# A hybrid encoder layer on one core: G leaves in quarters of a stage, and two stages of it stay in SBUF

## The chip, the cores and the metric

The kernel runs on one core of a Trainium2 chip. The metric is the device time in microseconds (us) of one execution, lower is better; the median of three runs before the change is 1501.55 us (1500.29 to 1506.06). The engines are TensorE (PE, matmuls), VectorE (DVE), ScalarE (ACT), GpSimd (POOL) and SyncE (SP, which here only issues transfers). ScalarE and GpSimd issue transfers too, each on a queue of its own, and all queues share the core's 16 DMA engines.

## The reference, cut to what matters

One encoder layer over 512 tokens of width 1024: layer norm, two kinds of attention, an output projection, layer norm, and then PEER, a feed-forward layer that picks experts by product keys. The change touches PEER alone.

```python
q = (xb @ w_q).reshape(PEER_CHUNK, PEER_HEADS, PEER_KEY_DIM)
s1 = jnp.einsum('thd,kd->thk', q[..., :half], sub_keys[0])
s2 = jnp.einsum('thd,kd->thk', q[..., half:], sub_keys[1])
...                      # top 16 of each, top 16 of the 16 x 16 sums
idx = (e1 * PEER_N_KEYS + e2)            # 128 experts a token, of 16384
g = jax.nn.softmax(cv, axis=-1)
u = u_table[idx]
act = g * gelu(jnp.einsum('td,ted->te', xb, u))
return jnp.einsum('te,ted->td', act, v_table[idx])
```

U and V have 16384 rows of 1024 floats. A last layer norm follows.

## The kernel before, in words

The 512 tokens are four chunks of 128. Chunk 0 is done **by gathers**: for each of its 128 picks, GpSimd gathers a row of U per token into a tile (`gat`, eight buffers), VectorE multiplies it with h and sums (`gather_u`, line 1564, into the scratch tile `scr`), and later the same with rows of V (`gather_v`, line 1575).

Chunks 1 to 3 are done **densely**: the table is taken as 128 blocks of 128 experts. Per block, `hidden = gelu(h @ U_block)`, times a dense weight matrix G, and the product times `V_block` is summed in PSUM over all blocks (`expert_out`, line 1590). G has one weight for each token and expert, mostly zeros. It is built from one-hot matrices: for eight tokens at a time VectorE and ScalarE write one-hot tiles (`oh_i`, `oh_j`), PE multiplies them, and ScalarE copies the products from PSUM into a **stage tile** `g_st` of 32 tokens (128 partitions x 128 blocks x 32 tokens, 16 KB a partition, 2 MB in all). There are two stage tiles, `bs0` and `bs1`, used in turn. A full stage goes to `g_dram` in DRAM by one write issued on ScalarE's queue (lines 1124 and 1199). Chunks 2 and 3 are built by `build_g_split` (fp16, line 1075), chunk 1 last by `build_g` (line 1158). That makes twelve stages. Only the very last one (chunk 1, group 3) is not written: its tile `bs1` is kept and later read from SBUF.

Chunk 1 needs more than G: its 128 tokens are `own` tokens, whose hidden values are also had by gathers (`rows`, line 1237 the gather, line 1239 the product, in place, with five row buffers). These rows run beside the building of G.

**The order** is written out by hand. While G is built, PE also multiplies the first 104 blocks of U (`lead_block`, line 1349, tile `whole` holds h transposed) and the gate matrix. A generator `pe_work` yields this PE work in small pieces, and `run` (line 1458) goes through the steps of a builder: after each step that costs VectorE time it puts in as much PE work as fits (`run_pe`), and some rows (`own`). Every engine then works its own list in order. SP's list holds the loads of U blocks, of gate weights, the first load of G back from DRAM (line 1502, for eight blocks of experts and chunks 2 and 3), and then the loads of V blocks.

In the **last stage** (from about 903 us) each of the 128 blocks needs its V block, split in a high and a low part, and its piece of G: `load_g` (line 1517) fetches eight blocks of G at a time, in four loads of three 32-token groups each (`q` = 0 to 3); for `q` = 1 the group that stayed in `bs1` is copied by ScalarE (line 1527) and only two groups are loaded. The gathers of chunk 0 run beside it.

SBUF is full, so where tiles lie matters: a tile in a place that was used before waits for the last user of that place. After G is built, `pb.close()` frees `bt` (the one-hots) and `bs0`; the pools `pV` (V blocks, half of G's pieces) and `pO` (`a_hi`, `a_lo`, the two parts of the weighted hidden values) take this place from the inner end, so that `a_hi`, `a_lo` and the first V tile lie where `bs0` was. `pR.close()` frees the routing tiles, the row buffers and `raw_u`; `pG` (`scr` and the eight `gat`) takes their place. `whole` lies in a pool of its own and keeps its place to the end.

## Time and profile before

| | us |
|---|---|
| median of three runs | 1501.55 |
| fastest, slowest | 1500.29, 1506.06 |
| the profiled execution | 1503.96 |
| its span in the profile | 1502.0 |
| PE busy | 1464.8 |
| DVE busy | 1288.5 |
| ACT busy | 632.8 |
| POOL busy | 571.2 |

The times below are those of one profiled execution, counted from the start of its span. In a table by stage the columns are: the stage, its length, the busy time of each engine with its instructions, the clock that PE was granted (1.00 is full), the mean share of time in which the DMA engines were busy, and GB/s moved. In a timeline the columns are start, length, engine, line and operation, with the idle time ahead of it and what ended it in brackets. In a list of waits: who waited for whom, us in total, times, the longest. In a list of transfers: size and median us from issue to landing. The building of G covers about 490 to 900 us; its writes leave at 515, 537, 565 and 590 us (chunk 2), 748, 770, 797 and 813 us (chunk 3), 841, 862 and 877 us (chunk 1).

### The profile page before, as it was taken

The page shows a single profiled execution, that of the slowest core. Times are in us where ns is not written, and L with a number is a line of the kernel's source. Part 1 is how long each engine was busy: PE and PEld are TensorE (multiplying, and loading weights), DVE is VectorE, ACT ScalarE, POOL GpSimd, SP SyncE. Part 2 cuts the span into 40 slices and gives each one's busy share as a digit, 9 for nine tenths or more (in the row PEclk, how much of TensorE's full clock was granted, in tenths as well). Part 3 has the DMA queues.
Part 4 walks back from the last instruction along what each step waited for, and adds up shares of the span by engine and source line. Part 5 has one row for each costly group of instructions (what it writes and reads, how often), then busy time and mean ns, then how long its engine had stood idle before and what let it go on. Part 6 is the DMA issues. An engine that isn't in the chain of part 4 may idle for free.

```text
span 1502.0 us, 22685 instructions
## 1 busy us (share of the span) xinstructions
PE 1464.8 (98%) x7725; PEld 1231.3 (82%) x7725; DVE 1288.5 (86%) x2830; ACT 632.8 (42%) x1175; POOL 571.2 (38%) x520
## 2 busy tenths in 40 slices
PE   9999999999999989999999999999999999999997
PEld 5788777788888878788888988888988888888885
DVE  7376786579998979998767989999989999999997
ACT  3355676243221654212555663444434333333433
POOL 1013110010014544334432335555645666666630
PEclk9999999999999999999999999999999999999999
DMA  7343341175339999999999999999999999999992
GB/s 252 98 113 97 87 119 36 29 242 168 99 135 353 349 415 378 389 323 339 393 418 386 364 385 371 417 415 415 418 401 383 411 412 412 411 412 413 411 385 85
DMA packets 192294, 455.82 MB, mean 303 GB/s; under 512 B 18225, under 2 KB 96049, under 8 KB 190770
## 3 DMA queue, kind: packets, MB, share of 16 engines
q1 hardware_dynamic: 119936, 212.63, 38.7%
q0 software_dynamic: 57984, 207.12, 35.4%
q10 hardware_dynamic: 14258, 34.61, 5.9%
q8 instruction: 61, 1.00, 0.2%
q14 instruction: 55, 0.45, 0.1%
HBM read 412.62 MB, written 38.80 MB: 301 GB/s over the span
## 4 chain that ended last, share of the span: by engine, by line
PE 46%; issue 8%; DVE 6%; POOL 6%; DMA 4%; ACT 1%; POOLq 0%; ACTq 0%; DVEq 0%
PE acc L1590 34%; PE mm L1349 4%; DMA whi<-in_u_rows_dram,s_ix 3%; POOL whi L1237 2%; POOL wlo L1237 2%; PE hp L131 2%; PE hp L130 2%; PE hp L129 2%; PE tr L1178 1%; POOL row L1237 1%; PE hp L1349 1%; DMA g_dram<-g_st 1%; DVE whi L1239 1%; DVE wlo L1239 1%; DVE ci L887 0%
## 5 line engine op out<-in xcount | busy, mean ns | idle before, releaser
L1573 POOL DMA_INDIRECT gat<-in_v_rows_dram,i_sel x128 | 207.5, 1621 | 110.9 <-DVE base L1575 86.9
L1558 POOL DMA_INDIRECT gat<-in_u_rows_dram,i_sel x102 | 135.2, 1325 | 112.1 <-DVE hdot L1564 79.7
L110 ACT CAST a_hi<-gt 128x384 fp32r<-128x384 f32 (+2 forms) x128 | 65.0, 509 | 264.7 <-DVE gt L1640 162.8
L1575 DVE SCALAR_TENSOR_TENSOR base<-gat,hdot,base 128x1024 f32<-128x1024 f32 x128 | 163.9, 1280 | 1.8
L110 DVE TENSOR_TENSOR wlo<-raw,whi 128x1024 fp32r<-128x1024 f32 (+4 forms) x113 | 131.5, 1164 | 39.4 <-ACT whi L110 38.9
L110 ACT CAST whi<-raw 128x1024 fp32r<-128x1024 f32 (+4 forms) x113 | 113.0, 1001 | 90.6 <-PE mm L130 47.3
L1349 PE MATMUL mm<-whole,raw 128*128 128x256 f32 x656 | 149.2, 381 | 0.0
L1237 POOL DMA_INDIRECT whi<-in_u_rows_dram,s_ix x51 | 64.2, 1259 | 223.4 <-DVE cand L993 129.7
L1590 PE MATMUL acc<-hTh,a_hi 128*128 128x512 f32 x480 | 148.8, 390 | 0.0
L1590 PE MATMUL acc<-hTl,a_hi 128*128 128x512 f32 x480 | 148.6, 390 | 0.1
L1590 PE MATMUL acc<-hTh,a_lo 128*128 128x512 f32 x480 | 148.4, 389 | 0.0
L1349 PEld LDWEIGHTS mm<-whole,raw 128*128 128x128 f32 x656 | 122.9, 190 | 15.6
L1564 DVE CUSTOM_DVE_ANT_0 scr<-gat,h 128x1024 f32<-128x1024 f32 x102 | 124.6, 1222 | 2.0
L1590 PEld LDWEIGHTS acc<-hTl,a_hi 128*128 128x128 f32 x480 | 90.0, 188 | 19.5 <-DVE hTl L110 0.5
L1590 PEld LDWEIGHTS acc<-hTh,a_lo 128*128 128x128 f32 x480 | 90.1, 188 | 18.9
L110 ACT CAST hTh<-v_raw 128x1024 fp32r<-128x1024 f32 x78 | 81.9, 1050 | 55.3 <-PE acc L1590 19.9
L1590 PEld LDWEIGHTS acc<-hTh,a_hi 128*128 128x128 f32 x480 | 88.4, 188 | 17.1 <-ACT a_hi L110 0.2
L110 DVE TENSOR_TENSOR hTl<-v_raw,hTh 128x1024 fp32r<-128x1024 f32 x78 | 95.0, 1219 | 5.4 <-ACT hTh L110 5.4
L1237 POOL DMA_INDIRECT wlo<-in_u_rows_dram,s_ix x51 | 60.7, 1191 | 68.4 <-DVE s_dot L1239 55.8
L1590 PE MATMUL acc<-whi,a_hi 128*128 128x512 f32 x276 | 85.0, 389 | 0.0
L1590 PE MATMUL acc<-wlo,a_hi 128*128 128x512 f32 x276 | 85.0, 389 | 0.0
L1590 PE MATMUL acc<-whi,a_lo 128*128 128x512 f32 x276 | 84.9, 389 | 0.0
(414 smaller groups left out, 3524.0 us busy)
## 6 DMA issues: line engine op xcount, KB each, us to landing
v_raw<-in_v_rows_dram SPq DMA_DIRECT2D x82, 512.0 KB, 12.7
raw<-in_uT_dram SPq DMA_DIRECT2D x81, 512.0 KB, 8.2
g_dram<-g_st ACTq DMA_DIRECT2D x11, 2048.0 KB, 12.5
raw<-in_v_rows_dram SPq DMA_DIRECT2D x44, 512.0 KB, 13.3
gt<-g_dram SPq DMA_DIRECT2D x45, 384.0 KB, 13.7
ge_dram<-ge ACTq DMA_DIRECT2D x88, 128.0 KB, 6.9
ge<-ge_dram SPq DMA_DIRECT2D x88, 128.0 KB, 13.1
raw_u<-in_uT_dram SPq DMA_DIRECT2D x18, 512.0 KB, 7.5
```

Of the source, the lines that this page charges most:

```text
L110: cut = nc.scalar.copy(hi, src), nc.vector.tensor_tensor(lo, src, r32(hi), op=OP.subtract)
L129: nc.tensor.matmul(ps, a[0], b[0], start=start, stop=False)
L130: nc.tensor.matmul(ps, a[0], b[1], start=False, stop=False)
L131: nc.tensor.matmul(ps, a[1], b[0], start=False, stop=stop)
L1237: nc.gpsimd.indirect_dma_start(out=u[:], out_offset=None, in_=u_rows, in_offset=bass.IndirectOffsetOnAxis(ap=ix[:, k:k + 1], axis=0))
L1239: nc.vector.tensor_tensor_reduce(u, u, x, op0=OP.mult, op1=OP.add, accum_out=dots[:, k:k + 1], scale=1.0, scalar=0.0)
L1349: nc.tensor.matmul(ps[:, :N_U], raw[:, k], whole[:, k, :], start=(k == 0), stop=(k == 7))
L1558: nc.gpsimd.indirect_dma_start(out=u[:], out_offset=None, in_=u_rows, in_offset=bass.IndirectOffsetOnAxis(ap=i_sel[:, c, k:k + 1], axis=0))
L1564: nc.vector.tensor_tensor_reduce(scr, u, h[c], op0=OP.mult, op1=OP.add, accum_out=hdot[:, c, k:k + 1], scale=1.0, scalar=0.0)
L1573: nc.gpsimd.indirect_dma_start(out=u[:], out_offset=None, in_=v_rows, in_offset=bass.IndirectOffsetOnAxis(ap=i_sel[:, c, k:k + 1], axis=0))
L1575: nc.vector.scalar_tensor_tensor(base[c], u, hdot[:, c, k:k + 1], base[c], op0=OP.mult, op1=OP.add)
L1590: nc.tensor.matmul(acc[c][hf], a[:, cs], b[:, hf * 512:(hf + 1) * 512], start=(n == 0 and i == 0), stop=(n == 127 and i == 2))
```

## The change

- **Writes in quarters.** A finished stage is no longer written at once. Its four quarters (32 of the 128 blocks each, 512 KB, 4 KB a partition) go on a list, and a new function `send` issues one at the head of each step of `run`. What is left on the list is issued before the first load of G back, and once more at the end of the building.
- **Two stages stay.** Groups 2 and 3 of chunk 1 stay in `bs0` and `bs1`. `load_g` copies one of them for `q` = 0 and the other for `q` = 1, and loads two groups instead of three for both.
- **Places.** `bs0` is now kept to the end like `bs1` and lies beside it, so `bt` lies further in. `whole` is freed with the routing tiles. To that end the rest of `pe_work` is put in ahead of `pR.close()` (and of the first V loads). `pV` opens after it.
- **Gather tiles.** `scr` is gone: `gather_u` writes its product over the gathered row, and the last layer norms use a gather tile. The eight tiles are now 4 `gat`, 2 `gat_w` (where `whole` was) and 2 `gat_v`, taken in a fixed order: four, two, two. The two rows of layer-norm parameters at the end are loaded into `gat`.

The core of the diff:

```diff
+G_PARTS = 4
...
-    pW = ctx.enter_context(tc.tile_pool(name="pW", bufs=1, reuse_waits="tile"))
+    pR = ExitStack()
+    pW = pR.enter_context(tc.tile_pool(name="pW", bufs=1, reuse_waits="tile"))
     whole = pW.tile([128, 8, N_U], F32, name="whole")
...
+    bs = [ctx.enter_context(tc.tile_pool(name="bs0", bufs=1, side="right", reuse_waits="tile")), bs1]
     bt = pb.enter_context(tc.tile_pool(name="bt", bufs=2, side="right", reuse_waits="tile"))
-    bs = [pb.enter_context(tc.tile_pool(name="bs0", bufs=1, side="right", reuse_waits="tile")), bs1]
...
+    parts = []
+
+    def send():
+
+        if parts:
+            g, t, x = parts.pop(0)
+            n = 128 // G_PARTS
+            nc.scalar.dma_start(g_dram[g][:, x * n * GT:(x + 1) * n * GT],
+                                t[:, x * n:(x + 1) * n].rearrange("p i t -> p (i t)"))
...
-                if c == NGC and g == N_S // GT - 1:
+                if c == NGC and g >= N_S // GT - 2:
                     g_last.append(stage)
                 else:
-                    nc.scalar.dma_start(g_dram[g], stage.rearrange("p i t -> p (i t)"))
+                    parts.extend((g, stage, x) for x in range(G_PARTS))
...
         for amount in steps:
+            send()
...
+        while parts:
+            send()
         first_g = pX.tile([128, NTG, GB, GT], F32, name="gt1")
...
         for x in own:
             run_pe(x)
+        while parts:
+            send()
         pb.close()
...
-        g = slice(q * NTG // 4 + (q == 1), (q + 1) * NTG // 4)
-        if q == 1:
-            nc.scalar.copy(t[:, N_S // GT - 1], g_last[0][:, i:i + GB, :])
+        g = slice(q * NTG // 4 + (q == 1), (q + 1) * NTG // 4 - (q == 0))
+        if q < 2:
+            nc.scalar.copy(t[:, N_S // GT - 2 + q], g_last[q][:, i:i + GB, :])
...
+    with tc.manual_schedule(engines={nc.vector.engine, nc.scalar.engine, nc.tensor.engine, nc.sync.engine,
+                                     nc.gpsimd.engine}):
+        gating = True
+        for _ in pe_work:
+            pass
     pR.close()
...
-    scr = pG.tile([128, D], F32, name="scr")
+    def gat():
+        nonlocal n_gat
+        name, n = (("gat", GATS - 4), ("gat_w", 2), ("gat_v", 2))[max(0, n_gat % GATS // 2 - 1)]
+        n_gat += 1
+        return pG.tile([128, D], F32, name=name, bufs=n)
...
-        nc.vector.tensor_tensor_reduce(scr, u, h[c], op0=OP.mult, op1=OP.add, accum_out=hdot[:, c, k:k + 1],
+        nc.vector.tensor_tensor_reduce(u, u, h[c], op0=OP.mult, op1=OP.add, accum_out=hdot[:, c, k:k + 1],
```

## The prediction

> **What bounds the kernel now.** I read the page first, then busy time by stage, then the engine waits inside the stages that have idle time, then the transfers in flight there.

> ```profile
> span 1502.0 us, 22685 instructions
> PE 1464.8 (98%) x7725; PEld 1231.3 (82%) x7725; DVE 1288.5 (86%) x2830; ACT 632.8 (42%) x1175; POOL 571.2 (38%) x520
> ```

> TensorE is busy for 98% of the span, and the change takes no matmul away. All there is to win is the 37 us in which PE stands still, and the time in which it runs at a lower clock. The stages from the first write of G on:

> ```profile
> core 0: us, PE busy (x) PEld busy (x) DVE busy (x) ACT busy (x) POOL busy (x), PEclk, DMA share, GB/s
> 515.00:540.00 25.00, 25.00 (x164) 21.89 (x162) 18.04 (x30) 16.55 (x41) 11.18 (x9) 1.00 1.00 399
> 540.00:555.00 15.00, 10.08 (x63) 8.72 (x62) 8.51 (x14) 4.99 (x11) 4.25 (x4) 0.89 1.03 420
> ...
> 600.00:615.00 15.00, 14.08 (x63) 11.32 (x62) 13.16 (x51) 1.80 (x4) 3.82 (x4) 1.00 1.03 412
> ...
> 780.00:795.00 15.00, 11.90 (x55) 9.85 (x53) 10.71 (x17) 6.71 (x17) 5.96 (x5) 0.77 1.02 404
> ...
> 884.00:903.00 19.00, 16.48 (x93) 13.65 (x92) 14.48 (x36) 10.79 (x25) 5.62 (x7) 1.00 0.94 378
> 903.00:1480.00 577.00, 577.00 (x2814) 488.65 (x2814) 558.05 (x744) 225.25 (x316) 334.30 (x223) 1.00 1.01 398
> ```

> From 903 on PE never stops, so whatever is won before 903 arrives at the end in full. PE's idle time is 4.92 us in 540-555, 0.92 in 600-615, 3.10 in 780-795 and 2.52 in 884-903. The clock adds to it: 15 us at 0.89 lose 1.65, 15 us at 0.77 lose 3.45. Together 16.6 us, and that is the ceiling of the gain. The stalls themselves, in PE's timeline:

> ```profile
> 541.80 1.04 PE L1105 MATMUL tr<-oh_i,oh_j 128*128 128x128 f16 x15 [1.70 <-DVE oh_j L1144]
> ...
> 551.78 1.78 PE L1105 MATMUL tr<-oh_i,oh_j 128*128 128x128 f16 x15 [3.22 <-DVE oh_j L1144]
> ...
> 787.29 0.29 PE L1105 MATMUL tr<-oh_i,oh_j 128*128 128x128 f16 x1 [2.79 <-DVE oh_j L1144]
> ```

> PE waits for one-hot products of VectorE. VectorE is late because, in order, it first multiplies rows of U that GpSimd gathers (L1239), and these arrive late. Its waits in 515-555, then in 750-790:

> ```profile
> DVE whi L1239 <- DMA whi<-in_u_rows_dram,s_ix: 5.5, 4, 3.4
> DVE row L1239 <- DMA row<-in_u_rows_dram,s_ix: 5.2, 2, 4.9
> DVE wlo L1239 <- DMA wlo<-in_u_rows_dram,s_ix: 2.7, 3, 1.6
> ```
> ```profile
> DVE wlo L1239 <- DMA wlo<-in_u_rows_dram,s_ix: 5.6, 4, 3.8
> DVE whi L1239 <- DMA whi<-in_u_rows_dram,s_ix: 4.9, 4, 1.9
> DVE row L1239 <- DMA row<-in_u_rows_dram,s_ix: 1.5, 1, 1.5
> ```

> That is 13.4 and 12.0 us of lateness, of which PE felt 4.92 and 3.10: about 8.5 us are absorbed by VectorE's lead over PE. Time from issue to landing, one line each from the transfers of 500-515 (before the first write of G), then from those of 520-550 and 740-790 (with such writes):

> ```profile
> whi<-in_u_rows_dram,s_ix POOLq DMA_INDIRECT x4, 6.1
> ```
> ```profile
> whi<-in_u_rows_dram,s_ix POOLq DMA_INDIRECT x4, 15.0
> ```
> ```profile
> g_dram<-g_st ACTq DMA_DIRECT2D x2, 2048.0 KB, 12.9
> ...
> whi<-in_u_rows_dram,s_ix POOLq DMA_INDIRECT x7, 12.9
> ```

> A row takes 6.1 us in the quiet and 13 to 15 beside the writes. The last stall, at 884-903, is of another kind:

> ```profile
> 877.25 0.33 ACTq L1199 DMA_DIRECT2D g_dram<-g_st  x1
> ...
> 889.71 0.41 ACT L110 CAST a_hi<-gt 128x256 fp32r<-128x256 f32 x1 [5.00 <-DMA g_dram<-g_st]
> ```
> ```profile
> 890.15 0.43 DVE L110 TENSOR_TENSOR a_lo<-gt,a_hi 128x256 fp32r<-128x256 f32 x1 [2.81 <-ACT a_hi L110]
> ```
> ```profile
> 892.01 2.53 PE L1178 MATMUL tr<-oh_i,oh_j 128*128 128x128 f32 x16 [1.19 <-ACT g_st L1191]
> ...
> 898.23 1.17 PE L1178 MATMUL tr<-oh_i,oh_j 128*128 128x128 f32 x8 [1.00 <-DVE oh_j L1220]
> ```

> The tile of a_hi lies where stage tile bs0 was, so ScalarE stands 5.0 us until the last 2 MB of G have left bs0; the copies out of PSUM queue behind it, and PE loses 2.4 us.

> **The change part by part.**

> *The last stall.* Group 2 of chunk 1 is no longer written, bs0 stays, and pO and pV move to where raw_u, row and bt were. Those are read for the last time by 878 (PE, raw_u), by 886 (VectorE, row) and, for bt, by the last products. So nothing holds a_hi after 878: the 5.0 us go, and with them 2.2 of the 2.52 us. The v loads, in SP's order

> ```profile
> 889.74 10.52 SPq L1543 DMA_DIRECT2D v_raw<-in_v_rows_dram  x3
> ```

> start with the first at about 886 instead of 889.74 and the others with the last products, as now; PE needs them only after the two blocks that are cut early. The tail of pe_work that now stands ahead of them issues nothing on SP any more. Gain 2.2 us, bounds 1.5 and 2.5.

> *Four writes for one.* 11 writes become 40: one 512 KB quarter at the head of each of the next four steps. The bytes fall by one stage.

> ```profile
> DMA packets 192294, 455.82 MB, mean 303 GB/s; under 512 B 18225, under 2 KB 96049, under 8 KB 190770
> ```

> Only 1524 packets are 8 KB or more, 1408 of them (11 x 128) these writes, at 16 KB; rows of U and V go in 4 KB. How far do the rows profit? Lower bound, nothing: the engines are full (399 to 420 GB/s in the stages above, no less than the 398 of the last stage), and what is full is not sped up by cutting it smaller. Upper bound, all 14.0 us (6.57 + 0.92 + 6.55). Between them: 2.10 MB in 12.9 us are 163 GB/s, 39% of 417; three queues served alike would leave a write a third, 139. The 24 GB/s set free go mostly to the rows. How fast these go, from VectorE's time on line 1239 (two instructions a row) between the writes and in 724-748, where VectorE was ahead and PE set the pace:

> ```profile
> 515.00:552.50 37.50, 14.13 (x24) 0.99 1.01 406
> 724.00:748.00 24.00, 13.48 (x22) 1.00 1.01 395
> ```

> 12 rows in 37.5 us, one in 3.1 or 168 GB/s, where PE asks for one in 2.2. With 24 GB/s more it is one in 2.7: the lateness per row falls from 0.9 to 0.5 us, by some 40%. It does not vanish, but since 8.5 of 13.4 us are absorbed already, a fall by 37% (4.92 of 13.4) in the first set and by 26% (3.10 of 12.0) in the second is enough to keep PE running. The writes themselves may end later: each stage tile has a whole stage of time. I take 65% of the two large stalls with their clock, 0.65 x 13.1 = 8.5 us, and half of the 0.92, because the estimate stands only just above the threshold.

> [...]

> [...]

> *ScalarE issues 29 more writes.*

> ```profile
> L1124 ACTq DMA_DIRECT2D g_dram<-g_st x8: 326/326/327, 515.5 to 813.3; - x8
> ```

> 29 x 0.33 = 9.5 us on ScalarE, which is 66% busy in 515-540 and mostly waits for PE. Behind a quarter queue its share of the one-hots and the copies out of PSUM. Cost 0 to 3 us; I take 0.8, since no engine waits for ScalarE in the large stalls. There is a second wait in it. The program hands the transfers of SP and ScalarE eight completion semaphores in turn, so an issue waits for the eighth before it, which SP already shows on loads of U that touch neither tensor:

> ```profile
> SPq L1309 <- DMA ge_dram<-ge: 3.2, 1, 3.2
> SPq L1309 <- DMA g_dram<-g_st: 2.8, 1, 2.8
> ```

> With four quarters inside one round of eight tokens, that eighth is, by my estimate from the rate of loads and writes, about 9 us old instead of 16. This is rival 3.

> *The first load of G back (L1502)* waits for all writes of chunks 2 and 3.

> ```profile
> SPq L1502 <- DMA g_dram<-g_st: 8.4, 1, 8.4
> ```
> ```profile
> 826.15 0.38 SPq L1502 DMA_DIRECT2D gt<-g_dram  x1
> 826.62 1.01 SPq L1309 DMA_DIRECT2D raw<-in_uT_dram  x2
> ```

> The last stage's first quarter leaves at 813.3 as now, the other three only after the lag of lead blocks, at about 818. No gathers run there, the same bytes remain, so I expect the load at 826 to 828. Behind it queue two loads of U, the first needed about 2 us after it lands. Cost 0 to 3 us, I take 0.5.

> *The rest costs nothing.*

> ```profile
> L1564 DVE CUSTOM_DVE_ANT_0 scr<-gat,h 128x1024 f32<-128x1024 f32 x102 | 124.6, 1222 | 2.0
> L1239 DVE CUSTOM_DVE_ANT_0 whi<-whi,h_s 128x1024 f32<-128x1024 f32 x51 | 62.1, 1218 | 18.2 <-DMA whi<-in_u_rows_dram,s_ix 18.2
> L1527 ACT COPY gt<-g_st 128x256 f32<-128x256 f32 x15 | 6.0, 402 | 1.6 <-DVE a_lo L110 1.3
> ```

> Writing the product over u instead of scr: 1218 against 1222 ns, the in-place form being L1239's. 15 more copies of 402 ns lie on ScalarE in the last stage, 39% busy (225 of 577); if PE were to wait for them it would be 6 us. 15 loads of G shrink by a third, which PE does not feel. The fifth and sixth gathers now wait for PE's last reading of whole (about 896) and the eighth for h_s as now; their products are due after 910, a landing of 8 us fits.

> *Sum:* 2.2 + 8.5 + 0.5 - 0.8 - 0.5 = 9.9 us. The profiled execution took 1503.96 us, 1502.0 of span and 1.96 around it, 2.4 above the median of 1501.55. From its own time the sum gives 1494.1, on the scale of the median **1491.7**.

> **The rivals.**
> 1. *The rows are freed wholly.* 16 KB packets are the whole cause; landing falls to 6-8 us, all 16.6 us come back, less 1.3 for issues: 1486.2. For it: 6.1 against 15.0. Against: the landing stays long at full bandwidth.
> 2. *The DMA engines are simply full.* Rows stay at 13 us, PE stalls as before at 550 and 787, and only the 2.2 us less 1.3 remain: 1500.7. For it: 399-420 GB/s. Against: writes may be late and rows may not.
> 3. *Slower: ScalarE blocks on completions.* A quarter, in order, waits for a transfer 9 us old; at the landing of 12.9 it waits 3.9 us, 31 us over the eight stages of chunks 2 and 3. It decides once wait and issues in a stage exceed ScalarE's idle third, some 7 us of 21. Then the stalls of today remain and each set gets another like them: +13.1 - 2.2 = 1512.5.

> **How the numbers follow.** Forecast 0.48, rival 1 0.13, rival 2 0.29, rival 3 0.10. What a measurement of this kernel tells from no change is about 0.5%, 7.5 us: faster is below 1494.0, slower above 1509.1. The forecast's own range is 1487 to 1496, three quarters of it below 1494: 0.36 + 0.13 + 0.02 of rival 2 = 0.51 faster; slower 0.08 of rival 3; 0.41 the same. The range 1485 to 1503 holds forecast, rivals 1 and 2 and leaves out rival 3.

> **What would show it.** In the profile after: rows of U landing at about 11 us beside the quarters; no PE wait above 2 us and a clock of 1.00 in the stages that stood at 0.89 and 0.77; no ScalarE wait for g_dram before a_hi; PE at the last stage some 10 us earlier than 903. I am wrong if rows still take 13 us and more, if ScalarE's queue shows waits for transfers, or if PE gets idle time after it enters the last stage.

## The result and the profile after

| | before | after |
|---|---|---|
| median | 1501.85 | 1492.91 |
| fastest, slowest of six runs | 1500.29, 1506.06 | 1491.66, 1495.41 |
| the profiled execution, its span | 1503.96, 1502.0 | 1492.1, 1490.3 |
| ratio with its 95% interval | | 0.9939 [0.9924, 0.9954] |

The changed kernel is 8.9 us faster. The prediction was 1491.7 in a range of 1485 to 1503. The head of the page after:

```profile
span 1490.3 us, 22670 instructions
...
PE 1459.5 (98%) x7725; PEld 1228.6 (82%) x7725; DVE 1285.3 (86%) x2830; ACT 635.5 (43%) x1190; POOL 575.5 (39%) x520
```

Between the two profiled executions lie 11.7 us of span. To place them, first busy time from 490 us to the stage's end, before and then after (columns as in the prediction):

```profile
490.00:1480.00 990.00, 975.43 (x5100) 835.48 (x5099) 909.68 (x1512) 416.20 (x764) 500.59 (x366) 0.99 1.00 389
```
```profile
490.00:1468.30 978.30, 969.77 (x5094) 832.41 (x5093) 903.46 (x1509) 417.18 (x773) 503.16 (x364) 1.00 0.99 388
```

PE idles 14.57 us in the first and 8.53 in the second: **6.0 us less idle time**. The rest is clock. In stretches of 5 us, before:

```profile
550.00:555.00 5.00, 3.22 (x19) 2.94 (x20) 3.95 (x7) 1.58 (x3) 1.95 (x2) 0.66 1.04 413
...
785.00:790.00 5.00, 2.39 (x17) 2.13 (x18) 4.19 (x7) 0.89 (x2) 1.88 (x3) 0.70 1.03 416
790.00:795.00 5.00, 5.00 (x16) 4.08 (x15) 4.42 (x8) 2.26 (x7) 3.15 (x3) 0.62 1.00 380
```

and after:

```profile
555.00:560.00 5.00, 4.55 (x25) 3.97 (x26) 4.04 (x8) 4.16 (x12) 1.49 (x2) 0.66 1.03 415
```

While G is built, before loses 1.7 us of clock at 550 and 1.5 + 1.9 at 785, after only 1.7 at 555: **3.4 us less loss**. About 1.7 us more come from the clock in the stretch at 175 to 190, long before the change acts (0.94, 0.50 and 0.88 before, one 0.67 after); the two executions merely differ there. So 6.0 + 3.4 = 9.4 us belong to the change, beside 8.9 in the medians. The last 0.6 us lie before 490 as well, in PE's idle time there (12.83 and 12.28 us).

What PE waits for in 490 to 905, before and after:

```profile
PE tr L1105 <- DVE oh_j L1144: 9.3, 5, 3.2
PE tr L1178 <- ACT g_st L1191: 1.5, 2, 1.2
...
PE tr L1178 <- DVE oh_j L1220: 1.2, 2, 1.0
```
```profile
PE tr L1115 <- DVE oh_j L1154: 2.8, 3, 1.6
PE hp L1359 <- ACT ge L1341: 2.8, 2, 2.3
PE tr L1188 <- DVE oh_j L1230: 1.0, 1, 1.0
```

Waits for one-hots fall from 10.5 to 3.8 us. One wait has grown, PE's for a `ge` of ScalarE (from 0.6 to 2.8 us); the only clock drop of that part follows it, in PE's timeline after:

```profile
555.45 1.22 PE L1359 MATMUL hp<-whole,gt 128*128 128x256 f32 x2 [2.29 <-ACT ge L1341]
...
782.79 1.04 PE L1115 MATMUL tr<-oh_i,oh_j 128*128 128x128 f16 x15 [1.13 <-DVE oh_j L1154]
...
797.82 1.11 PE L1115 MATMUL tr<-oh_i,oh_j 128*128 128x128 f16 x16 [1.55 <-DVE oh_j L1154]
...
886.18 1.22 PE L1188 MATMUL tr<-oh_i,oh_j 128*128 128x128 f32 x8 [1.01 <-DVE oh_j L1230]
```

VectorE's waits for gathered rows in 490 to 905, before and after:

```profile
DVE whi L1239 <- DMA whi<-in_u_rows_dram,s_ix: 15.4, 11, 3.4
DVE wlo L1239 <- DMA wlo<-in_u_rows_dram,s_ix: 9.8, 9, 3.8
DVE row L1239 <- DMA row<-in_u_rows_dram,s_ix: 8.1, 5, 4.9
```
```profile
DVE whi L1249 <- DMA whi<-in_u_rows_dram,s_ix: 12.7, 13, 1.6
DVE wlo L1249 <- DMA wlo<-in_u_rows_dram,s_ix: 10.1, 11, 1.6
...
DVE row L1249 <- DMA row<-in_u_rows_dram,s_ix: 3.7, 6, 1.2
```

The sum falls only by a fifth, 33.3 to 26.5 us. The longest single wait falls from 4.9 to 1.6: the rows are nearly as late as before, but evenly so.

### The profile page after: what moved, and what is told of

Read it like the earlier page. It is cut to its first block, busy times and chain, and to the rows that moved or that the text cites. A ratio compares the mean times of both kernels' runs of the same rounds, so it can differ in the third digit from the quotient of the medians.

```text
span 1490.3 us, 22670 instructions
## 1 busy us (share of the span) xinstructions
PE 1459.5 (98%) x7725; PEld 1228.6 (82%) x7725; DVE 1285.3 (86%) x2830; ACT 635.5 (43%) x1190; POOL 575.5 (39%) x520
## 5 line engine op out<-in xcount | busy, mean ns | idle before, releaser
L1359 PEld LDWEIGHTS mm<-whole,raw 128*128 128x128 f32 x656 | 122.7, 190 | 15.6
L1602 POOL DMA_INDIRECT gat<-in_v_rows_dram,i_sel x64 | 103.9, 1624 | 53.6 <-DVE base L1604 42.3
L1619 PEld LDWEIGHTS acc<-hTh,a_hi 128*128 128x128 f32 x480 | 88.4, 188 | 17.1 <-ACT a_hi L111 0.3
L1587 POOL DMA_INDIRECT gat<-in_u_rows_dram,i_sel x52 | 70.8, 1362 | 43.2 <-DVE hdot L1593 30.8
L1604 DVE SCALAR_TENSOR_TENSOR base<-gat,hdot,base 128x1024 f32<-128x1024 f32 x64 | 82.0, 1281 | 0.9
L1249 DVE CUSTOM_DVE_ANT_0 whi<-whi,h_s 128x1024 f32<-128x1024 f32 x51 | 62.1, 1218 | 15.2 <-DMA whi<-in_u_rows_dram,s_ix 15.2
```

Source lines behind the costliest of these rows:

```text
L1249: nc.vector.tensor_tensor_reduce(u, u, x, op0=OP.mult, op1=OP.add, accum_out=dots[:, k:k + 1], scale=1.0, scalar=0.0)
L1359: nc.tensor.matmul(ps[:, :N_U], raw[:, k], whole[:, k, :], start=(k == 0), stop=(k == 7))
L1587: nc.gpsimd.indirect_dma_start(out=u[:], out_offset=None, in_=u_rows, in_offset=bass.IndirectOffsetOnAxis(ap=i_sel[:, c, k:k + 1], axis=0))
L1602: nc.gpsimd.indirect_dma_start(out=u[:], out_offset=None, in_=v_rows, in_offset=bass.IndirectOffsetOnAxis(ap=i_sel[:, c, k:k + 1], axis=0))
L1604: nc.vector.scalar_tensor_tensor(base[c], u, hdot[:, c, k:k + 1], base[c], op0=OP.mult, op1=OP.add)
L1619: nc.tensor.matmul(acc[c][hf], a[:, cs], b[:, hf * 512:(hf + 1) * 512], start=(n == 0 and i == 0), stop=(n == 127 and i == 2))
```

## The experiments

Each kernel computes the whole output. The table holds the median, the ratio to the kernel before (run beside it) and, from views of the waits in 490 to 905, VectorE's waits for rows (sum, longest) and PE's waits for one-hots and for ScalarE. The last column has PE's whole idle time in 490 to 905 and the number of windows of 3.41 us that it ran there at half clock, each worth 1.7 us (the last section shows these windows).

| kernel | writes of a stage | median | ratio [95%] | rows | PE for one-hots | PE for ScalarE | PE idle, windows at half clock |
|---|---|---|---|---|---|---|---|
| before | 1, 16 KB packets | 1501.85 | | 33.3, 4.9 | 10.5 | 2.3 | 14.6, 3 |
| after | 4, 4 KB, spread | 1492.91 | 0.9939 [0.9924, 0.9954] | 26.5, 1.6 | 3.8 | 3.9 | 8.5, 1 |
| after, again | the same | 1494.75 | 0.9953 [0.994, 0.9967] | 26.5, 1.7 | 3.2 | 5.3 | 8.9, 1 |
| writes only | the same | 1492.56 | 0.9939 [0.992, 0.9958] | 24.9, 2.2 | 1.5 | 6.4 | 9.1, 1 |
| writes only, again | the same | 1491.41 | 0.9936 [0.9917, 0.9956] | 24.6, 2.1 | 5.4 | 3.7 | 9.8, 0 |
| places only | 1, 16 KB | 1499.07 | 0.9983 [0.997, 0.9997] | 34.8, 5.1 | 9.7 | 1.1 | 12.7, 1 |
| halves | 2, 8 KB, spread | 1495.49 | 0.9954 [0.9937, 0.997] | 31.7, 3.1 | 9.6 | 1.1 | 11.7, 1 |
| halves, 4 KB | 2, 4 KB, spread | 1498.87 | 0.998 [0.9965, 0.9996] | 26.0, 2.1 | 9.0 | 1.1 | 10.6, 2 |
| one, 4 KB | 1, 4 KB | 1500.45 | 0.9985 [0.9971, 0.9999] | 24.8, 2.1 | 2.5 | 8.8 | 12.2, 3 |
| four at once | 4, 4 KB, together | 1500.54 | 0.9995 [0.9984, 1.0006] | 26.6, 2.5 | 1.0 | 10.5 | 12.5, 2 |
| eighths | 8, 2 KB, spread | 1505.49 | 1.0025 [1.0016, 1.0034] | 5.7, 1.8 | 0.9 | 15.6 | 17.1, 3 |
| by partition | 4, 16 KB, spread | 1509.5 | 1.005 [1.0033, 1.0066] | 25.6, 3.1 | 5.2 | 14.8 | 20.0, 4 |

The profiled execution lies within 2.7 us of its kernel's median, except for places only and four at once (3.8 and 4.4 below it) and for e6 further down (4.1 above). The last column tells nearly all of the differences: the time of the profiled execution less PE's idle time and 1.7 us for each window is 1480 to 1485 us in all twelve, where these times themselves run from 1491 to 1510.

### Which half of the change pays

Places only (e1_whole) takes the changed kernel and leaves the writes whole (each issued at the head of the next step):

```diff
-G_PARTS = 4
+G_PARTS = 1
```

> The changed kernel with a stage in one write again (16 KB packets, 2 MB), everything else of the change kept: two stages on chip, the new places, the gather tiles. Theory A (packets: a 16 KB packet holds a DMA engine four times as long as a row's 4 KB packet, so rows come late) and theory B (pacing: four smaller transfers spread over the steps leave room for the rows between them) both expect the row lateness and the stalls at 550 and 787 to be back with the clock loss, and only the last stall gone: 1499.5 (1498 to 1501). Theory C (the gain is the last stall and the second stage on chip, the writes do nothing): 1493.

Measured 1499.07. The writes carry most of the gain. On theory A's packets: in the trace of the kernel before, the 1408 packets of 16 KB of the writes took 0.63 us each in the mean, the 50176 of 4 KB on GpSimd's queue, which carries the rows, 0.17 us. The old stalls are back in the trace:

```profile
PE tr L1115 <- DVE oh_j L1154: 9.7, 8, 2.8
```

Writes only (e8_writes_only) is the other half: the kernel before, eleven written stages, old places, with this.

```diff
-                    nc.scalar.dma_start(g_dram[g], stage.rearrange("p i t -> p (i t)"))
+                    parts.extend((g, stage, x) for x in range(G_PARTS))
...
         for amount in steps:
+            send()
```

> The kernel before with the quarter writes alone: four writes of 512 KB for each of eleven stages, all places, gather tiles and loads as before, the stage in bs0 still written and a_hi still in its place. Additive: the writes bring 1499.07 - 1492.91 = 6.2 us, so 1495.7 (1494 to 1497.5), and the stall of ScalarE ahead of a_hi is there. Rival (the quarters land later in the last stage, so this stall grows): 1498 to 1501.

Measured 1492.56, better than both expectations. The wait of `a_hi` for the stage tile is still there, but PE, whose longest pause at that place is 0.78 us, hardly feels it:

```profile
884.84 0.41 ACT L111 CAST a_hi<-gt 128x256 fp32r<-128x256 f32 x1 [3.37 <-DMA g_dram<-g_st]
```

So the halves don't add: some 2.5 us for the places with whole writes (0.17%), none beside cut ones. To be sure of that, both kernels ran once more, side by side (f3_after_again, f4_writes_only_again).

> The changed kernel as it is, beside the kernel that has the four writes alone. If the stage kept on chip and the new places add nothing once the writes are cut, both times agree within 1.5 us (1491.5 to 1493.5). If they keep the 2.5 us that they brought with whole writes, this one is 2 to 3 us faster than the other.

> The kernel before with the four writes a stage alone, beside the changed kernel. If the stage kept on chip and the new places add nothing, 1491.5 to 1493.5 us, within 1.5 us of the changed kernel. If they keep their 2.5 us, 2 to 3 us more than the changed kernel.

1494.75 and 1491.41, neither within the 1491.5 to 1493.5 that was expected: the places keep nothing of their 2.5 us. The simpler kernel came out faster both times, by 0.4 and by 3.3 us, but the intervals overlap, so whether it really is isn't settled.

### What the quarters do: packets, size, spread

Halves (e4_halves) set `G_PARTS = 2`.

> A stage in two writes of 1 MB with 8 KB packets. Theory A: half of the packet effect, fewer waits for completions, 1494 to 1497. Theory B: half of the pacing, 1496. It tells whether the size of the step matters, not A from B.

1495.49. The rows hardly gain (31.7 against 33.3 us), and TensorE still waits 9.6 us for one-hots, yet three quarters of the gain are there (0.46 of 0.61%); in this trace two of its three longest pauses (1.6 us at 541 and 2.3 at 792) cost no clock, where both sets of pauses before had cost some (the last section shows why).

One write with 4 KB packets (e3_one_4k): `g_dram` is laid out in quarters, so that a single write of 2 MB goes in packets of 4 KB.

```diff
-    g_dram = dram.tile([NTG, 128, 128 * GT], F32, name="g_dram")
+    g_dram = dram.tile([NTG, G_CUT, 128, 128 // G_CUT * GT], F32, name="g_dram")
...
+            nc.scalar.dma_start(g_dram[g].rearrange("c p x -> p c x"),
+                                t.rearrange("p (c i) t -> p c (i t)", c=G_CUT))
```

> One write for a stage, but with 4 KB packets: g_dram is laid out in quarters, so the one write has 512 runs of 4 KB. No pacing, 10 issues instead of 40, so few waits for completions on ScalarE and SyncE. Theory A: as the changed kernel or better by what those waits cost there (ScalarE's 2.29 us stall of PE and the clock after it, about 4 us): 1489 to 1493. Theory B: 1499.5, as with one write of 16 KB packets.

The rows are relieved as in the changed kernel (24.8 us), and the time is 1500.45 all the same. ScalarE waits 22.2 us for writes of G in 490 to 905, 10.0 of them ahead of a one-hot. Its timeline there, and then PE's waits of 490 to 905:

```profile
550.25 0.39 ACT L1342 ACTIVATE ge<-mm 128x256 f32<-128x256 f32 x1
560.29 0.33 ACTq L1344 DMA_DIRECT2D ge_dram<-ge  x1
560.67 1.31 ACT L1147 ACTIVATE oh_i<-iota,eT 128x128 f16<-128x128 f32 x4 [10.03 <-DMA g_dram<-g_st]
```
```profile
PE hp L1360 <- ACT ge L1342: 5.5, 2, 4.9
PE tr L1116 <- ACT g_st L1129: 3.0, 2, 2.8
```

A one-hot (`oh_i`) uses nothing of `g_dram`. What waited is the issue ahead of it: `ge` was ready at 550.64, and the write of it left at 560.29. The trace's records give the completion semaphore of each transfer. This one has number 100, which the write of G issued at 540.96 had before it, and all transfers of SyncE and ScalarE share eight numbers in turn: in the trace of the kernel before, a number comes back with the eighth issue after it in 574 of 612 cases, with the seventh or ninth in the others, and in all 535 cases with a known landing the transfer that had it last has landed before the issue. That is the mechanism of rival 3. All five of ScalarE's waits for transfers in this part end so, with an issue that leaves 0.4 us ahead of the waiting instruction. The stall has moved from VectorE to ScalarE.

Four at once (f1_at_once): the changed kernel, with all quarters issued when the stage is full.

```diff
                     parts.extend((g, stage, x) for x in range(G_PARTS))
+                    while parts:
+                        send()
```

> The changed kernel, but the four quarters of a stage (512 KB, 4 KB packets) are issued one behind the other as soon as the stage is full, none waits for a step. If the packet size alone brings the gain, VectorE's waits for rows in 490-905 stay near 25 us, TensorE's waits for one-hots near 3 us, and the time is 1492 to 1494 us. If the pacing is needed, the last quarter lands some 16 us after the stage, as the single write of 4 KB packets did, ScalarE and SyncE again wait 10 us and more for writes of G, and the time is 1498 to 1501 us.

1500.54: nothing is left of the gain, although the rows stand at 26.6 us and the one-hots at 1.0. PE waits for ScalarE instead, 10.5 us in all, most of it here:

```profile
PE tr L1115 <- ACT g_st L1128: 7.4, 3, 3.0
```

The same packets, the same size, the same number of issues: **the spread alone is worth 5.8 us** against the changed kernel run beside it. Two writes of 4 KB packets (e5_two_4k) join the layout above with `G_PARTS = 2`.

> The changed kernel with a stage in two writes of 1 MB that have 4 KB packets (g_dram laid out in quarters, two of them in a write). Theory A2 (small packets relieve the rows whatever the number of writes; what they cost is waits for completions, since an issue of ScalarE or SyncE waits for the eighth transfer before it, and a write that lands late blocks there): rows as little late as with one write of 4 KB packets, a landing of 12 to 14 us and so next to no waits of ScalarE for transfers, 1490 to 1494. Theory B2 (the size of a write counts): as the two halves with 8 KB packets, 1495.5.

1498.87, a miss for both. The rows are relieved (26.0 us), ScalarE waits for no write beyond 1.5 us, and yet PE waits 9.0 us for one-hots. Why the same lateness reaches PE here and not with four quarters stays open.

Eighths (f2_eighths): `G_PARTS = 8`, 2 KB packets.

> The changed kernel with eight writes of 256 KB and 2 KB packets a stage, one at each step. If a smaller packet leaves the rows still more of the queues, VectorE's waits for rows fall from 26.5 to about 20 us and the time is 1489 to 1492 us. If the completions in turn are now the bound, 40 more issues make a round of eight shorter in time, SyncE's waits for writes of G rise well above 37 us and ScalarE's above 11 us, TensorE gets waits for loads of U or for ge, and the time is 1495 to 1499 us.

1505.49, slower than before and beyond both ranges, and the clearest picture of the trade. Waits of VectorE, ScalarE and PE:

```profile
DVE oh_i L1142 <- PE tr L1115: 27.4, 14, 6.4
```
```profile
ACT g_st L1128 <- DMA g_dram<-g_st: 13.2, 7, 3.0
...
ACT g_st L1128 <- DMA ge_dram<-ge: 10.2, 5, 3.3
```
```profile
PE tr L1115 <- ACT g_st L1128: 13.5, 8, 5.1
```

VectorE's waits for rows sum to only 5.7 us, but this sum can't be set beside the others: VectorE itself stands 27.4 us behind PE (1.8 us in the changed kernel), and the rows have that time to land. They do land sooner, after 9.6 to 10.7 us instead of 12.2 to 12.7 with quarters (medians of the three row tiles, gathers of 515 to 560), at 411 to 413 GB/s, no less than with other packets. The price is ScalarE's, and it is the turn again: an issue leaves right ahead of each copy into the stage tile that waits here. One wait of 4.39 us, at 885, has no issue ahead of it; there the copy can only wait for the stage tile to be read.

By partition (e2_by_partition) cuts a stage the other way: four spread writes of 32 partitions each, with the old 16 KB packets.

```diff
-            nc.scalar.dma_start(g_dram[g][:, x * n * GT:(x + 1) * n * GT],
-                                t[:, x * n:(x + 1) * n].rearrange("p i t -> p (i t)"))
+            nc.scalar.dma_start(g_dram[g][x * n:(x + 1) * n, :],
+                                t[x * n:(x + 1) * n].rearrange("p i t -> p (i t)"))
```

> Four writes of 512 KB at the same steps as in the changed kernel, but cut by partitions (32 partitions of 16 KB each) instead of by blocks: the same sizes, issues and pacing, with 16 KB packets. Theory A: the gain of the writes is lost, 1499 to 1503 (the waits for completions stay). Theory B: as the changed kernel, 1493.

1509.5, the slowest of all and beyond both ranges, though its writes land soonest (8.0 us). ScalarE waits for loads that SyncE issued:

```profile
ACT oh_i L1146 <- DMA g_raw<-in_gate_w_dram: 10.2, 1, 10.2
ACT g_st L1128 <- DMA raw_u<-in_uT_dram: 6.4, 1, 6.4
```

Again an issue of `ge_dram` leaves 0.4 us ahead of the waiting instruction, so these are waits for the turn. What makes those loads late is not shown. The run changes packets and partitions together, so it says nothing clean about packets; its rows land after 13.4 to 14.0 us, as beside whole writes with such packets (13.4 to 13.9 before).

### Can ScalarE be freed of the turn

Both kernels move the issue of the 88 small `ge_dram` writes from ScalarE to SyncE: e6_ge_on_sync in the changed kernel, e7_one_4k_ge_on_sync in the one with a single write of 4 KB packets.

```diff
-            nc.scalar.dma_start(ge_dram[i], ge)
+            nc.sync.dma_start(ge_dram[i], ge)
```

> The changed kernel with one more edit: the 88 writes of hidden values (ge_dram) are issued by SyncE instead of ScalarE. The waits for the eighth transfer then fall on SyncE, whose loads run ahead. Theory A2: ScalarE's waits for transfers (11 us in 490 to 905) and PE's stall of 2.3 us behind one of them go, with the clock loss after it: 1488 to 1491. Rival: SyncE is blocked instead, the loads of U come late and PE waits for them: 1493 to 1498.

> One write of 4 KB packets per stage as before (1500.45), and the writes of hidden values on SyncE. It tests whether ScalarE's 22 us of waits for transfers were what took the gain of the small packets there. Theory A2: these waits go, 1489 to 1494. Rival (a write that lands after 16.8 us is too slow in itself, or SyncE now blocks the loads of U): 1497 to 1502.

1498.81 (0.9986 [0.9975, 0.9998]) and 1499.65 (0.9989 [0.9977, 1.0001]): both go the rival's way, the first 0.8 us past its range. In the first, SyncE now waits for the data of each of these writes and holds the loads behind it, and PE waits for blocks of U, which it did not in the changed kernel:

```profile
SPq L1343 <- ACT ge L1341: 61.6, 18, 5.1
```
```profile
PE mm L1359 <- DMA raw_u<-in_uT_dram: 1.7, 1, 1.7
...
PE mm L1359 <- DMA raw<-in_uT_dram: 1.2, 1, 1.2
```

That is the smaller part. ScalarE isn't freed either: by this trace it waits 51.0 us for transfers in 490 to 905 (11.7 in the changed kernel), and PE 8.6 us for ScalarE. In the second kernel PE waits 3.0 us for blocks of U and only 2.1 for ScalarE, and its idle time there is 8.5 us, as in the changed kernel; half clock explains 3.4 of the 7.5 us between the two profiled executions (1.7 of them before 490), and what costs the rest is not shown.

## Why the prediction was right, point by point

**The bound** held: PE never stands still in the last stage. The row before covers 905 to 1480, the row after the same stretch of work (575 us, 2806 and 2808 matmuls), 12 us earlier where 10 were predicted; 1.7 of the 12 are the clock at 175 to 190:

```profile
905.00:1480.00 575.00, 575.00 (x2806) 487.04 (x2805) 556.08 (x741) 225.19 (x315) 332.88 (x222) 1.00 1.01 398
```
```profile
893.00:1468.30 575.30, 575.30 (x2808) 487.40 (x2807) 552.27 (x742) 228.74 (x329) 336.31 (x223) 1.00 1.00 396
```

**Four writes, +9.0.** This term carried the forecast, and the runs bear it out: the writes alone bring 9 to 10 us by their ratios. The quicker rows were sized well. VectorE's time on the rows, in the stretch where 12 rows came before:

```profile
515.00:552.50 37.50, 17.05 (x27) 1.00 1.03 413
```

13.5 rows in 37.5 us are one in 2.8; predicted was one in 2.7. That three queues served alike would leave a write a third was the author's supposition, not shown before the change. Measured by queue, ScalarE's moved 43% of the bytes beside whole writes (537 to 550 and 565 to 578 before) and 33% with quarters in flight (518 to 531 and 562 to 577 after); the other two were not alike there (GpSimd's 38 and 52%, SyncE's 29 and 15%). A row beside the quarters of 520 to 550 lands after 12.6 us in the changed kernel's second run (15.0 before; about 11 predicted), and a quarter after 13.3, so a stage as a whole ends later, as said:

```profile
g_dram<-g_st ACTq DMA_DIRECT2D x4, 512.0 KB, 13.3
...
whi<-in_u_rows_dram,s_ix POOLq DMA_INDIRECT x4, 12.6
```

What failed in this step is the threshold. It compared sums: lateness had to fall by 37% and 26% before PE would run through. In the same two sets it fell by 28% and 14% (13.4 to 9.6 and 12.0 to 10.3 us), and PE's waits for one-hots still fell by 64% over the whole part. What changed with it is the longest wait, 4.9 to 1.6 us: by these two traces VectorE's lead covers many short waits and not a long one. It isn't the rule, since halves with 4 KB packets have no row wait above 2.1 us and PE waits 9.0; what the rule is stays open. The step also gave all credit to the packets, and four at once shows that they alone don't bring the time.

**The last stall, +2.2,** was mis-sized. The 5.0 us of `a_hi` are gone: it runs at 871.42 without a wait. But PE's idle time at the end of the building falls only from 2.52 to 1.76 us, before and after:

```profile
882.00:905.00 23.00, 20.48 (x111) 17.03 (x110) 18.45 (x46) 11.39 (x26) 8.72 (x9) 1.00 0.94 373
```
```profile
870.00:893.00 23.00, 21.24 (x119) 18.23 (x118) 19.92 (x48) 12.62 (x29) 9.59 (x9) 1.00 0.79 284
```

The term had booked the 1.00 us for `oh_j` as a consequence of ScalarE's wait. It stands unchanged as 1.01. Measured 0.8, not 2.2, and beside cut writes worth nothing in the time.

**ScalarE's issues, -0.8.** Also mis-sized, and here the forecast was lucky to come out at 1491.7. "No engine waits for ScalarE in the large stalls" held for the kernel before. After, one-hots and copies on ScalarE wait 9.7 us for transfers that they don't use. The wait that reaches PE isn't among them, because the first trace has no landing times and puts it down to VectorE (4.73 us ahead of the one-hot at 553.15). The second run has them. ScalarE's timeline there:

```profile
547.61 0.39 ACT L1341 ACTIVATE ge<-mm 128x256 f32<-128x256 f32 x1
552.32 0.33 ACTq L1343 DMA_DIRECT2D ge_dram<-ge  x1
552.69 1.31 ACT L1146 ACTIVATE oh_i<-iota,eT 128x128 f16<-128x128 f32 x4 [4.70 <-DMA ge_dram<-ge]
...
554.57 0.36 ACT L1341 ACTIVATE ge<-hp 128x256 f32<-128x256 f32 x1
```

The issue of one `ge_dram` write waits until another, issued at 539.07 with the same completion semaphore (109), has landed. The `ge` that PE needs comes behind it. PE pays 2.29 us at 555 in the first run and 1.63 in the second, each with 1.7 us of clock behind it: some 4 us. The two errors, -1.4 and -3.2 us, are made up by the writes: what is left of 9.4 for them is 9.4 - 0.8 + 4.0 = 12.6 of the 14.0 us that were their upper bound.

**The first load of G, -0.5.** It leaves at 816.14 instead of 826.15, with the general advance: no cost.

**The rivals.** Rival 1 (rows freed wholly) fell: rows still land after 12 us and more. Rival 2 (engines full) fell too, and its argument with it: the rate is as high as before (411 to 415 GB/s with quarters of 512 KB, 399 to 420 with whole writes), and the rows still land sooner, with 2 KB packets after 9.6 to 10.7 us where it was 13.4 to 13.9 (gathers of 515 to 560). What made eighths slow is the waits and not the rate (411 to 413 GB/s). Rival 3 was put at 0.10 and is real: the changed kernel pays a small part of it, four at once pays the whole gain, and eighths are slower than before by it. Its point of decision, though, was named wrongly. ScalarE's idle share doesn't settle it: in writes only ScalarE waits 22.6 us for transfers, in its second run 30.4, and both are among the fastest. In the traces the price came where one long wait stood just ahead of a `ge` or a copy that PE needs: pauses of PE of 2.96 us in four at once, 4.91 in one with 4 KB, 5.10 in eighths.

**The signs.** Of the signs that the prediction named for itself, rows stayed slower than the 11 us (12.6), one PE wait is above 2 us (2.29), and the clock is 1.00 in the two stages that stood at 0.89 and 0.77 but falls at 555. One of the signs of being wrong came true: ScalarE's queue does show waits for transfers. The forecast time holds; the step on ScalarE's issues does not.

## What to carry to other kernels

When a large transfer starves small ones that an engine needs in order, cut it and spread the pieces over the steps of the work: cutting it and issuing the pieces together won nothing here, and cutting it further cost more in completions than it won in rows. Count what each further issue makes its own queue wait for. And judge a change by the idle time of the engine that bounds the kernel, not by the sum of the waits ahead of it: VectorE's waits for rows stand at 25 to 27 us in kernels that took from 1491 to 1510 us. Two gains need not add, so try each half of a change alone (here the cut writes do all).

## What the runs showed of the hardware that was not expected

```profile
548.03:551.44 3.41, 0.53 (x4) 0.17 (x2) 1.55 (x3) 0.26 (x1) 0.05 (x1) 1.00 0.99 399
551.44:554.85 3.41, 3.07 (x19) 2.80 (x20) 2.39 (x4) 1.49 (x3) 1.75 (x2) 0.50 1.04 412
```
```profile
790.69:794.11 3.42, 1.93 (x20) 1.83 (x21) 3.42 (x7) 1.08 (x2) 1.15 (x1) 1.00 1.03 417
794.11:797.52 3.41, 3.41 (x18) 3.00 (x17) 3.41 (x7) 1.22 (x4) 1.16 (x1) 1.00 1.06 432
```

  So a pause of 2.27 us in halves cost no clock, as an edge of the grid cut it in two, and one of 1.63 us in the changed kernel's second run did, as its window had 2.22 us of idle time in all. After a window at half clock less was enough once: with 0.65 us of idle time the clock stayed at half (786.96 to 790.37 before).
- **A transfer's completion held an engine that doesn't use it.** In the kernel with one write of 2 MB in 4 KB packets, ScalarE stood 10.0 us ahead of a one-hot that doesn't touch `g_dram`, until such a write had landed. The records show eight completion semaphores for all transfers of SyncE and ScalarE, given out in turn (in the kernel before, the same one again with the eighth issue in 574 of 612 cases); no run here changed their number.
- **Rows landed sooner beside smaller packets, at the same rate,** 406 to 416 GB/s throughout. One row tile, from the gathers of 515 to 560, in places only (16 KB packets), halves (8 KB), the changed kernel's second run (4 KB) and eighths (2 KB):

```profile
whi<-in_u_rows_dram,s_ix POOLq DMA_INDIRECT x6, 15.3
```
```profile
whi<-in_u_rows_dram,s_ix POOLq DMA_INDIRECT x6, 14.8
```
```profile
whi<-in_u_rows_dram,s_ix POOLq DMA_INDIRECT x7, 12.2
```
```profile
whi<-in_u_rows_dram,s_ix POOLq DMA_INDIRECT x6, 10.7
```

  In the kernel before it took 13.6 us and by partition 13.9, so 16 and 8 KB aren't told apart.
